# Gates, latents and rope key as two more pairs of tiles with seven part products

## The chip, the cores and the metric

The kernel runs on one core of one Trainium2 chip. The metric is the device time of that core in microseconds (us) from launch to end. The engines are called as in the profile: PE (TensorE, matmul; PEld its weight loads), DVE (VectorE), ACT (ScalarE), POOL (GpSimd) and SP (SyncE, whose queue issues all transfers here). Transfers run on 16 DMA engines.

## The reference

One layer of an encoder over 2048 tokens of width 1024, in float32. What matters here is its input projection:

```
xn   = rms_norm(x, ln_mix_g)                   # 2048 x 1024
proj = xn @ w_in                               # 1024 x 2512
q, k, v, o = proj in four parts of 512         # mLSTM: q and k go through a 3-tap convolution, o through a sigmoid
gates = proj[2048:2064] + b_gates              # 16 per token: input and forget gate, 2 directions, 4 heads
c_q   = rms_norm(proj[2064:2320], q_norm_g)    # latent of the attention queries
c_kv  = rms_norm(proj[2320:2448], kv_norm_g)   # latent of keys and values
k_rope = rotate(proj[2448:2512], cos, sin)     # 64, shared by the heads
```

Then come the chunkwise mLSTM in both directions, the latent attention, the output projection, a gated MLP with a convolution, and a per-layer input embedding.

## The kernel before

A float32 product is made of three products of float32r halves (low by high, high by low, high by high; `mm3`). A split is a cast of the high half on ACT and a subtraction on DVE (`split`, L117: L121 and L124).

**Input projection** (`in_proj`, L187). Loop over 16 tiles of 128 tokens. Per tile: load a tile of the turned x (L224), split it (`split_x`), multiply by the 464 columns of gates, latents and rope key (`nat` and `rest`, 24 matmuls of width 464, L134), multiply by the 512 value columns (`vals`, 24 of width 512), store the values to `v_d` (L294). `rest` scales on ACT, adds the gate bias, sums squares, rotates the rope key in 32-wide pieces on DVE; `finish` applies the norms; `turn_rest` turns the result by four transposes (L283) and stores it to `rest_d` (L288). Beside it run `square` (load rows of x, sum squares on ACT, L235 and L237), which gives the token factors `rcol`; `norm_row` turns eight of them into a row and stores it to `r_d`. From tile 4 on, three times per tile, a step of `work` is taken: `token_sums` (L398) loads x for a block of 1024 tokens, scales it by the row of factors (L429) and makes the token sums of the seven-product scheme, for both blocks; of the first block most are split into SBUF (`op`), the rest and all of the second go to `xo_d`.

**Pairs** (`pairs`, L506). For each of two blocks of 1024 tokens, six pairs of 128-feature tiles of q, k and o. A pair is a 2x2 product by Strassen's scheme: seven part products of 12 matmuls 128x512 each, 84 in all (`prod`, L544), in the banks `fx`, `fy`, `fz`, `fs`. `pair_load` loads the weights two pairs ahead, `pair_prep` makes their sums and splits them one pair ahead; `conv` applies the taps on DVE and the activation on ACT and stores. A function `side(at)` is called between part products and lets other work in: the gate calculation (`gates`, generator, pairs 1 to 4) and, in the last pair, the beginning of the queries (`queries_begin`; in each of two calls four plain-F32 matmuls 128x128, L713).

**What sets the order.** A scheduler orders each engine's instructions when the program is built, from the dependencies and the order of the code; each engine then runs its list in order and waits at semaphores. SP's list holds every transfer: one whose wait isn't met holds all behind it. The transfers take eight semaphores in turn, so that each also waits for the one eight places ahead of it.

## Time and profile before

| | us |
|---|---|
| median of 3 runs (lowest, highest) | 2844.04 (2841.64, 2844.45) |
| span of the profiled execution | 2844.3 |
| PE busy | 2810.8 |
| DVE, ACT, POOL busy | 2133.1, 1580.2, 212.2 |
| input projection, to the first pair's matmul | 189.8 |
| pairs, to the first matmul of the queries | 189.8 to 425.9 |

The page gives busy time per engine. In the rows of a timeline stand the start, the length, the engine, the line, what is written and read, the count and in brackets the idle time before, with what ended it. The pace of back-to-back instructions is the distance of their starts, which is less than the length of one, since they overlap. In the table by windows each row is a stretch of the span.

### The profile page before, as it was taken

The numbers are of one execution on the slowest core, as the hardware profiler recorded it, in microseconds if no ns is written. First come the engines' busy times: TensorE is split into PE (matmuls) and PEld (weight loads), VectorE is DVE, ScalarE is ACT, GpSimd is POOL, SyncE is SP. The second block draws the span as 40 slices with busy tenths as digits, with TensorE's granted clock in tenths as the row PEclk, the third lists the DMA queues.
The fourth block names the chain that finished last, engine by engine and source line by source line (L and its number), as shares of the span: only waits on it lengthen the run. The fifth ranks groups of instructions, "written<-read, shape, count | busy, mean of one in ns | idle before, by whom it ended". The sixth has DMA issues, their size and how long they took to land.

```text
span 2844.3 us, 39914 instructions
## 1 busy us (share of the span) xinstructions
PE 2810.8 (99%) x13932; PEld 2357.0 (83%) x13932; DVE 2133.1 (75%) x3673; ACT 1580.2 (56%) x3072; POOL 212.2 (7%) x331
## 2 busy tenths in 40 slices
PE   9999999999999999999999999999999999999998
PEld 8888888888888888888888888888888788888787
DVE  4877867777787777877778778777778766676777
ACT  6346775556556556655655556655556333254665
POOL 2100000000010000044100000000000000011012
PEclk9999999999999999999999999999999999999999
DMA  8874758554433333579745445567776757575864
GB/s 285 292 244 113 215 170 263 157 169 142 137 122 108 105 99 106 162 239 298 232 148 198 164 170 180 183 209 232 231 239 214 229 194 237 170 265 201 291 198 163
DMA packets 444529, 552.71 MB, mean 194 GB/s; under 512 B 34564, under 2 KB 296744, under 8 KB 444328
## 3 DMA queue, kind: packets, MB, share of 16 engines
q1 hardware_dynamic: 444328, 550.16, 60.2%
q8 instruction: 110, 1.80, 0.3%
q14 instruction: 91, 0.75, 0.1%
HBM read 357.45 MB, written 192.61 MB: 193 GB/s over the span
## 4 chain that ended last, share of the span: by engine, by line
PE 90%; DVE 4%; DMA 3%; issue 1%; ACT 1%; SPq 0%; POOL 0%; ACTq 0%; POOLq 0%; DVEq 0%
PE fy L1709 22%; PE fz L1709 15%; PE fx L1709 14%; PE bk L134 6%; PE ppv L1248 4%; PE tb L1236 3%; PE fy L544 3%; PE fx L544 2%; PE fz L544 2%; PE ppv L1249 2%; PE bk L1171 2%; PE bk L1173 2%; PE bk L1174 2%; PE bk L1172 2%; PE bk L1175 2%; PE fs L134 2%
## 5 line engine op out<-in xcount | busy, mean ns | idle before, releaser
L1709 PE MATMUL fz<-op,fw 128*128 128x512 f32 x1968 | 478.4, 391 | 2.4 <-DVE ug L1694 1.8
L1709 PE MATMUL fx<-op,fw 128*128 128x512 f32 x1968 | 475.9, 390 | 0.0
L1709 PE MATMUL fy<-op,fw 128*128 128x512 f32 x1968 | 475.1, 390 | 0.0
L1709 PEld LDWEIGHTS fz<-op,fw 128*128 128x128 f32 x1968 | 367.1, 188 | 81.1 <-DVE ug L1694 2.2
L1709 PEld LDWEIGHTS fy<-op,fw 128*128 128x128 f32 x1968 | 368.6, 188 | 76.9 <-DVE xt L1694 0.4
L1709 PEld LDWEIGHTS fx<-op,fw 128*128 128x128 f32 x1968 | 368.1, 188 | 76.1
L121 ACT CAST pt<-tb 128x512 fp32r<-128x512 f32 x256 | 146.9, 587 | 213.7 <-PE tb L1236 213.1
L1709 PE MATMUL fy<-op,fwd 128*128 128x512 f32 (+1 forms) x984 | 237.8, 390 | 1.5 <-DVE fh L1694 1.5
L1709 PEld LDWEIGHTS fy<-op,fwd 128*128 128x128 f32 x984 | 182.7, 188 | 39.7 <-DVE fh L1694 1.8
L1176 DVE TENSOR_REDUCE mx<-bk 128x1 f32<-128x512 f32 x256 | 175.2, 685 | 52.7 <-PE bk L1175 50.6
L124 DVE TENSOR_TENSOR pt<-tb,pt 128x512 fp32r<-128x512 f32 x256 | 173.1, 685 | 33.0 <-ACT pt L121 31.4
L1248 PE MATMUL ppv<-pt,kv 128*128 128x512 f32 x512 | 189.0, 407 | 1.0 <-DVE pt L124 1.0
L1193 ACT ACTIVATE pe<-bk,nm 128x512 f32<-128x512 f32 x256 | 174.5, 698 | 17.4 <-DVE nm L1187 15.6
L124 DVE TENSOR_TENSOR fw<-fwr,fw 128x1024 fp32r<-128x1024 f32 x124 | 150.9, 1220 | 35.3 <-ACT fw L121 35.0
L121 ACT CAST op<-opr 128x512 fp32r<-128x512 f32 x201 | 117.7, 620 | 73.0 <-DMA opr<-xo_d 13.2
L1236 PE MATMUL tb<-ident,pe 128*128 128x128 f32 x1024 | 150.9, 273 | 3.1 <-DVE pt L124 3.1
L121 ACT CAST fw<-fwr 128x1024 fp32r<-128x1024 f32 x124 | 129.8, 1050 | 37.5 <-DVE fwr L1683 20.0
L124 DVE TENSOR_TENSOR op<-opr,op 128x512 fp32r<-128x512 f32 x201 | 131.7, 692 | 19.0 <-ACT op L121 18.3
L1249 PE MATMUL ppv<-pt,kv 128*128 128x256 f32 x512 | 144.7, 283 | 0.0
L1236 PEld LDWEIGHTS tb<-ident,pe 128*128 128x128 f32 x1024 | 122.5, 140 | 23.4 <-DVE pt L124 5.4
L121 ACT CAST fw<-hraw 128x1024 fp32r<-128x1024 f32 (+1 forms) x72 | 70.1, 980 | 116.5 <-PE fx L1709 58.9
L1757 DVE SCALAR_TENSOR_TENSOR fgv<-uv,fcw,fgv 128x1024 f32<-128x1024 f32 x88 | 112.7, 1281 | 10.3 <-ACT fgv L1755 9.6
(409 smaller groups left out, 5200.8 us busy)
## 6 DMA issues: line engine op xcount, KB each, us to landing
fwr<-in_w_up SPq DMA_DIRECT2D x66, 512.0 KB, 4.7
fh<-h_d SPq DMA_DIRECT2D x48, 512.0 KB, 3.5
h_d<-fh SPq DMA_DIRECT2D x48, 512.0 KB, 4.3
s_d<-fwr SPq DMA_DIRECT2D x44, 512.0 KB, 3.2
fws<-s_d SPq DMA_DIRECT2D x44, 512.0 KB, 3.5
rw<-row_d SPq DMA_DIRECT2D x32, 512.0 KB, 5.2
tw_d<-tsum SPq DMA_DIRECT2D x60, 256.0 KB, 5.1
opr<-tw_d SPq DMA_DIRECT2D x60, 256.0 KB, 5.3
```

Of the source, the lines that this page charges most:

```text
L121: nc.scalar.copy(hi, src)
L124: (sub or nc.vector).tensor_tensor(lo, src, _f(hi), op=ALU.subtract)
L134: mm = lambda *a, **k: self.nc.tensor.matmul(*a, **k, skip_group_check=more)
L544: nc.tensor.matmul(out, a[:, k * P:(k + 1) * P], parts[lo], start=first, stop=lo == 1 and k == 3, skip_group_check=more)
L1171: mm(ps, ql, kh[:, ks], start=True, stop=False)
L1176: nc.vector.tensor_reduce(s.mx[:, kb:kb + 1], ps, axis=AX.X, op=ALU.max)
L1193: nc.scalar.activation(s.pe[:, kb % 2], s.banks[kb], AF.Exp, bias=s.nm, accum_out=s.rs[:, kb:kb + 1])
L1236: nc.tensor.transpose(t[:, j, :], s.p[kb][:, j * P:(j + 1) * P], self.ident)
L1248: mm(w.ps, vh[:, ks], pts[kb][:, j], start=kt == 0, stop=False, skip_group_check=True)
L1249: mm(w.ps[:, 0], vl[:, ks], pts[kb][:, j, 0], start=False, stop=kt == NT - 1, skip_group_check=True)
L1709: nc.tensor.matmul(out, a[:, k * P:(k + 1) * P], parts[lo][:, cols], start=first, stop=lo == 1 and k == last, skip_group_check=more)
L1757: nc.vector.scalar_tensor_tensor(t, u[:, tap:tap + 2 * SB], self.taps[:, tap, ct:ct + 1], t, op0=ALU.mult, op1=ALU.add)
```

## The change

The 464 columns leave the loop over token tiles. They become two more pairs per block, ahead of the six: the first holds the kv latent and, as its second tile, the first 64 columns (gates and 48 more) beside the 64 of the rope key; the second holds the two tiles of the query latent. A block has 8 pairs, 16 in all. Features now lie on partitions, so nothing is turned: a latent pair's `conv` stores u to `lat_d`, `kr_d` or `gate_d` and squares it; `sums` adds the squares over features by eight plain-F32 matmuls of one column against a constant; `norm_row` makes a row of factors from them (`lr_d`). In block two `rescale` reloads latents and rope key, applies factor and gain, rotates the key on POOL, turns the kv latent for `vv_d` (L699) and stores `rest_d`. `gates` reads its units straight from `gate_d` by 34 small transfers, and runs in pairs 12 to 14.

In the projection only `vals` is left per tile, with two `square`s per tile up to tile 8 and two steps of `work` from tile 5 on. `token_sums` makes the first block only, all but B22 split into SBUF; the second block's sums are in `next_sums`, taken in pairs 1 to 6 (by `side`).

Where the order of the lists moves, three places matter. First PE, at the end of the projection and the start of the pairs (`bk` is the projection's bank; `wsr` and `wsp` the weights of the rest and of the values). Before:

```order
L134 MATMUL bk<-wsr,xh 128x464 x24
L134 MATMUL bk<-wsp,xh 128x512 x30
L283 MATMUL rtp<-ident,nn 128x128 x4
L134 MATMUL bk<-wsp,xh 128x512 x18
L283 MATMUL rtp<-ident,nn 128x128 x4
L544 MATMUL fz<-op,fw_1851 128x512 x2
L629 MATMUL fy<-op,fw_1793 128x512
L544 MATMUL fx<-op,fw_1793 128x512 x4
L544 MATMUL fx<-op,fw_1794 128x512 x4
L544 MATMUL fx<-op,fw_1793 128x512 x4
L544 MATMUL fz<-op,fw_1851 128x512 x10
L544 MATMUL fy<-op,fw_2024 128x512 x4
```

Now:

```order
L139 MATMUL bk<-wsp,xh 128x512 x144
L300 MATMUL tb<-ident,rcol 8x128
L139 MATMUL bk<-wsp,xh 128x512 x120
L489 MATMUL fz<-op,fw_949 128x512 x7
L607 MATMUL fy<-op,fw_907 128x512
L489 MATMUL fx<-op,fw_907 128x512 x4
L489 MATMUL fx<-op,fw_908 128x512 x4
L489 MATMUL fx<-op,fw_907 128x512 x4
L489 MATMUL fz<-op,fw_949 128x512 x5
L489 MATMUL fy<-op,fw_1018 128x512 x4
```

The value tiles now follow each other without the products of width 464 and the transposes between them, and five matmuls instead of ten stand between `fx` and the `fy` that reads its copy.

Second, SP's queue where the first token loads (`xsr`) and the row of factors (`rrow`) are issued, up to the load of x tile 7 (the last row). Before:

```order
L235 DMA x_row<-in_x 128x1024 x3
L412 DMA xsr<-in_x_turned 128x1024
L148 DMA rrow<-r_d 128x1024
L412 DMA xsr<-in_x_turned 128x1024
L288 DMA rest_d<-rt 512x1x128
L412 DMA xsr<-in_x_turned 128x1024 x2
L420 DMA xo_d<-xsr 128x512
L294 DMA v_d<-vo 128x512
L277 DMA vv_d<-nn 128x128
L224 DMA x_t<-in_x_turned 128x8x128
```

Now:

```order
L240 DMA v_d<-vo 128x512
L303 DMA r_d<-r_439 8x128
L334 DMA xsr<-in_x_turned 128x1024 x2
L240 DMA v_d<-vo 128x512
L153 DMA rrow<-r_d 128x1024
L334 DMA xsr<-in_x_turned 128x1024 x2
L212 DMA x_t<-in_x_turned 128x8x128
```

The value store just ahead of x tile 7 was that of tile 4 and is now that of tile 5 (the second `v_d` row).

Third, DVE between two subtractions of x tiles (`xh<-x_t,xh`) while the first block's token sums are made. Before, around tile 7:

```order
L459 TENSOR_TENSOR xsr<-xsr 128x512
L269 TENSOR_TENSOR nn<-sc_848 128x32
L293 TENSOR_SCALAR vo<-bk,rcol 128x512
L270 COPY nn<-nn 128x64
L274 SCALAR_TENSOR_TENSOR nn<-rs,rsr,gn 128x256
L124 TENSOR_TENSOR xh<-x_t,xh 128x1024
L124 TENSOR_TENSOR op<-xsr,op 128x512
L450 TENSOR_TENSOR xsr<-xsr 128x512
L124 TENSOR_TENSOR op<-xsr,op 128x512
L253 TENSOR_TENSOR gt<-rs,bg 128x8 x2
```

Now, from tile 8 to tile 9:

```order
L129 TENSOR_TENSOR xh<-x_t,xh 128x1024
L354 TENSOR_TENSOR xsr<-xsr 128x512
L129 TENSOR_TENSOR op<-xsr,op 128x512
L350 SCALAR_TENSOR_TENSOR xsr<-xsr,gcol,rrow 128x1024
L129 TENSOR_TENSOR op<-xsr,op 128x512
L350 SCALAR_TENSOR_TENSOR xsr<-xsr,gcol,rrow 128x1024
L357 TENSOR_TENSOR xsr<-xsr 128x512
L129 TENSOR_TENSOR op<-xsr,op 128x512
L359 TENSOR_TENSOR xsr<-xsr 128x512
L129 TENSOR_TENSOR op<-xsr,op 128x512
L363 TENSOR_TENSOR xsr<-xsr 128x512
L129 TENSOR_TENSOR xh<-x_t,xh 128x1024
```

The small operations of `rest` and `finish` are gone, and whole quarters of the token sums stand between one tile's subtraction and the next.

The diff, cut to its core:

```diff
@@ in_proj @@
-        def rest(st, ps):
-            whole = self.at(f"t{st % 2}", [P, NREST], name="rs")
-            nc.scalar.activation(whole, ps[:, :NREST], AF.Copy, scale=rcol[:, st:st + 1])
-            for i, o in ((0, st), (8, NT - 1 - st)):
-                nc.vector.tensor_tensor(self.gt[:, i:i + 8, o], whole[:, i:i + 8], bg[:, i:i + 8], op=ALU.add)
-            rs = whole[:, 16:NREST]
-            sc = self.at(next(srot), [P, 6, 32], name="sc6")
-            nc.sync.dma_start(sc[:, 0:2], d["rope"][st * P:(st + 1) * P])
-            cos, sin, tt = sc[:, 0], sc[:, 1], sc[:, 2:6]
-            nn = nq[st] = self.at(f"t{2 + st % 2}", [P, 512], name="nn")
-            ssq = self.stat(2, "ssq2")
...
-        def vals(st):
-            ps = nat(st, wv, 512)
-            t = self.at("t4", [P, 512], name="vo")
-            nc.vector.tensor_scalar(t, ps, rcol[:, st:st + 1], None, op0=ALU.mult)
+                self.mm3(ps, x[:, 0, kt], x[:, 1, kt], wv[kt][:, 0], wv[kt][:, 1], kt == 0, kt == KT - 1)
+            t = self.at(f"t{4 + st % 2}", [P, 512], name="vo")
+            if st < 5:
+                nc.vector.tensor_scalar(t, ps, rcol[:, st:st + 1], None, op0=ALU.mult)
+            else:
+                nc.scalar.activation(t, ps, AF.Copy, scale=rcol[:, st:st + 1])
             nc.sync.dma_start(self.v_d[st], t)
...
         work = chain(self.token_sums(), self.pair_begin())
-        for st in range(2, NT):
+        sq = iter(range(1, NT))
+        for st in range(1, NT):
+            if st + 1 < NT:
+                load_x(st + 1)
+                split_x(st + 1)
+            for _ in range(2):
+                if (q := next(sq, None)) is not None:
+                    square(q)
...
+            vals(st)
+            if st == 4:
+                x_row_factors(0)
+            if st == 10:
+                x_row_factors(1)
                 self.pair_load(0)
-            if st + 2 < NT:
-                load_x(st + 2)
-            if st + 1 < NT:
-                split_x(st + 1)
-            rest(st, nat(st, wr, NREST))
-            if st < 5:
-                for q in range(4 * st - 4, 4 * st):
-                    square(q)
-            if st > 3:
+            if st > 4:
                 next(work, None)
...
+    NPB = 8
+    COLS = [(OFF_R + 272, None), (OFF_R + 16, OFF_R + 144)] + [(256 * j, 256 * j + P) for j in (0, 1, 2, 3, 6, 7)]
+    def load_w(self, t, j, e):
+        c = self.COLS[j][e]
+        for o, n, c in ((0, P, c),) if c is not None else ((0, 64, OFF_R), (64, 64, OFF_R + 400)):
+            self.nc.sync.dma_start(t[:, :, o:o + n], self.d["w_in"][0, :, c:c + n].rearrange("(k p) c -> p k c", p=P))
...
@@ token_sums @@
+        rr = self.row_bcast(self.at("x11", [P, 2 * SB], name="rrow"), self.r_d[0:2 * SB], 2 * SB)
+        yield
+        for k in range(4):
             a, b = nxt
-            if i < 7:
-                nxt = load(i + 1)
+            if k < 3:
+                nxt = load(k + 1)
             for t, kt in ((a, k), (b, k + 4)):
-                nc.vector.scalar_tensor_tensor(t, t, self.gcol[:, kt:kt + 1], rr[:, blk], op0=ALU.mult, op1=ALU.mult)
-            store(blk, "B22", k, b[:, H])
-            if blk:
-                store(blk, "B11", k, a[:, L])
-                store(blk, "B21", k, b[:, L])
-                yield
-                tt(a[:, H], a[:, H], a[:, L], op=ALU.subtract)
-                store(blk, "T1", k, a[:, H])
-                c = self.at(("u2", "w3")[k % 2], [P, 2, SB], name="xsc")
-                tt(c[:, 0], b[:, H], a[:, H], op=ALU.subtract)
-                store(blk, "T2", k, c[:, 0])
-                yield
-                tt(c[:, 1], c[:, 0], a[:, L], op=ALU.subtract)
-                store(blk, "T3", k, c[:, 1])
-                t4 = self.at("t7", [P, SB], name="xsd")
-                tt(t4, b[:, L], c[:, 0], op=ALU.subtract)
-                store(blk, "T4", k, t4)
-                yield
-                continue
+                nc.vector.scalar_tensor_tensor(t, t, self.gcol[:, kt:kt + 1], rr, op0=ALU.mult, op1=ALU.mult)
+            self.store_op(0, "B22", k, b[:, H])
...
+    def next_sums(self):
+        nc = self.nc
+        tt = nc.vector.tensor_tensor
+        rr = []
+        for e in range(2):
+            t = self.at(f"t{4 + e}", [P, SB], name="rrow")
+            rr.append(self.row_bcast(t, self.r_d[(2 + e) * SB:(3 + e) * SB], SB))
+        for k in range(4):
+            q = []
+            for i in range(4):
+                q.append(self.at(f"t{i}", [P, SB], name="xsq"))
+                nc.sync.dma_start(q[i], self.d["x_turned"][:, k + i // 2 * 4, (2 + i % 2) * SB:(3 + i % 2) * SB])
+            al, ah, bl, bh = q
+            def scale(t, i):
+                kt = k + i // 2 * 4
+                nc.vector.scalar_tensor_tensor(t, t, self.gcol[:, kt:kt + 1], rr[i % 2], op0=ALU.mult, op1=ALU.mult)
+            yield
+            scale(al, 0)
+            self.store_op(1, "B11", k, al)
+            scale(ah, 1)
+            tt(ah, ah, al, op=ALU.subtract)
+            self.store_op(1, "T1", k, ah)
+            yield
+            scale(bh, 3)
+            self.store_op(1, "B22", k, bh)
+            t2 = self.at("t7", [P, SB], name="xsd")
+            tt(t2, bh, ah, op=ALU.subtract)
+            self.store_op(1, "T2", k, t2)
+            yield
+            scale(bl, 2)
+            self.store_op(1, "B21", k, bl)
+            tt(al, t2, al, op=ALU.subtract)
+            self.store_op(1, "T3", k, al)
+            yield
+            tt(bl, bl, t2, op=ALU.subtract)
+            self.store_op(1, "T4", k, bl)
...
@@ pairs @@
+            if s.pr < 0:
+                u = u[:, 1:1 + 2 * SB]
+                if s.pr == -2 and half:
+                    nc.sync.dma_start(self.kr_d[:, ts], u[64:P])
+                    nc.sync.dma_start(self.gate_d[:, ts], u[0:16])
+                    return
+                nc.sync.dma_start(self.lat_d[2 if s.pr == -2 else half, :, ts], u)
+                s.sq[half] = sq = self.at(("w7", "w11")[half], [P, 2 * SB], name="lsq")
+                nc.scalar.activation(sq, u, AF.Square)
+                if s.pr == -1 and not half:
+                    tt(sq, sq, s.sq[1], op=ALU.add)
+                return
             if s.pr > 3:
...
+        def sums(s, bank):
+            ps = bank[:, 0:8]
+            for t in range(8):
+                nc.tensor.matmul(ps[:, t:t + 1], s.sq[0][:, t * P:(t + 1) * P], self.nhalf[:, 0:1], start=True, stop=True)
+            ssq = self.stat(8, "lssq")
+            nc.vector.tensor_copy(ssq, ps)
+            s.rc = self.rsq(ssq, 8, -2.0 / (P if s.pr == -2 else 2 * P))
...
+                if j in (2, 3) and at == 1:
+                    sums(lat[j - 2], bank)
+                if j in (2, 3) and at == 2:
+                    self.norm_row(bank[0:8, 0:P], lat[j - 2].rc, self.lr_d[j - 2], blk)
+                if 0 < i < 6 and at % 2:
+                    next(ahead, None)
+                if (i, at) == (6, 1):
+                    for _ in ahead:
+                        pass
+                if NPB < i < NPB + 4:
+                    next(scaled, None)
+                if NPB + 4 <= i < NPB + 7 and at != 3:
                     next(gates, None)
-                if i == 11:
-                    self.queries_begin(at, prev.spare if at % 2 else s.spare)
+                if i == N - 1:
+                    self.queries_begin(at, bank)
...
@@ rescale @@
+    def rescale(self, blk):
+        nc, d = self.nc, self.d
+        V, G = nc.vector, nc.gpsimd
+        halves = [slice((2 * blk + h) * SB, (2 * blk + h + 1) * SB) for h in range(2)]
+        def load(tag, src):
+            t = self.at(tag, [P, SB], name="rsp")
+            nc.sync.dma_start(t, src)
+            return t
+        def scale(t, n, row):
+            V.scalar_tensor_tensor(t, t, self.lgain[:, n:n + 1], row, op0=ALU.mult, op1=ALU.mult)
+            nc.sync.dma_start(self.rest_d[:, n, ts], t)
+        for ts in halves:
+            row = self.row_bcast(self.at("t5", [P, SB], name="rrow"), self.lr_d[0][ts], SB)
+            kv = load("t0", self.lat_d[2, :, ts])
+            cos, sin = [load(f"t{2 + i}", d["rope_keys"][:, i, ts]) for i in range(2)]
+            a, b = [self.at(("t1", "t4")[i], [P, SB], name="rsk") for i in range(2)]
+            both = lambda p: self.kr_d[p:p + 32, ts].unsqueeze(0).broadcast_to([2, 32, SB])
+            for e in range(2):
+                for t, p in ((a, 32 * e), (b, 32 - 32 * e)):
+                    for r in range(2):
+                        nc.sync.dma_start(t[64 * r + 32 * e:64 * r + 32 * e + 32], self.kr_d[p:p + 32, ts])
+            yield
+            scale(kv, 2, row)
+            G.tensor_tensor(a, a, cos, op=ALU.mult)
+            G.tensor_tensor(b, b, sin, op=ALU.mult)
+            G.tensor_tensor(a, a, b, op=ALU.add)
+            nc.sync.dma_start(self.rest_d[:, 3, ts], a)
+            yield
+            pt = self.gate_bank.rearrange("p (k t) -> p k t", t=P)
+            for k in range(4):
+                nc.tensor.transpose(pt[:, k], kv[:, k * P:(k + 1) * P], self.ident)
+            o = self.at("t7", [P, 4, P], name="vvo")
+            nc.scalar.copy(o, pt)
+            nc.sync.dma_start(self.vv_d[:, ts.start // P:ts.start // P + 4], o)
+            yield
+        for ts in halves:
+            row = self.row_bcast(self.at("t5", [P, SB], name="rrow"), self.lr_d[1][ts], SB)
...
@@ gates @@
+        raw = []
+        for f in range(2):
+            g = tl()
+            for r in range(2):
+                src = self.gate_d[8 * r + 4 * f:8 * r + 4 * f + 4].rearrange("h (c t) -> c h t", t=P)
+                for c in range(NT) if r else (None,):
+                    if r:
+                        nc.sync.dma_start(g[64 + 4 * (NT - 1 - c):64 + 4 * (NT - c)], src[c])
+                    else:
+                        nc.sync.dma_start(g[0:64], src)
+            raw.append(g)
         def to_units(f):
-            g = tl()
-            V.tensor_copy(g.rearrange("p (r c h) -> p r h c", r=2, h=4), gt[:, :, f])
-            yield
-            pt = pbank()
-            nc.tensor.transpose(pt, g, self.ident)
             o = tl()
-            flip(o, pt)
+            flip(o, raw[f])
+            V.tensor_scalar(o, o, self.gbias[:, f:f + 1], None, op0=ALU.add)
...
```

229 lines of the change are left out of this document (80 added, 149 removed).

## The prediction

> **What bounds the kernel now.** I read the page first, for the engines and the clock.
>
> ```profile
> span 2844.3 us, 39914 instructions
> PE 2810.8 (99%) x13932; PEld 2357.0 (83%) x13932; DVE 2133.1 (75%) x3673; ACT 1580.2 (56%) x3072; POOL 212.2 (7%) x331
> PEclk9999999999999999999999999999999999999999
> ```
>
> TensorE (PE) is busy for all but 33 us of the span, at full clock. So the time changes in two ways only: by PE work that goes or comes, and by new holes in PE. Everything the change touches lies in the first 426 us (the input projection and the pairs), so the table by windows comes next: length, then PE, PEld, DVE, ACT, POOL busy, clock, DMA share, GB/s.
>
> ```profile
> 20.00:40.00 20.00, 20.00 (x96) 16.99 (x95) 10.64 (x32) 11.97 (x24) 5.73 (x12) 1.00 0.81 257
> 80.00:120.00 40.00, 37.27 (x178) 31.52 (x177) 36.03 (x82) 17.61 (x39) 3.53 (x8) 1.00 0.90 283
> 120.00:160.00 40.00, 40.00 (x190) 34.16 (x190) 30.13 (x71) 9.54 (x22) 6.56 (x7) 1.00 0.98 319
> 200.00:240.00 40.00, 40.00 (x178) 32.85 (x177) 28.26 (x58) 22.39 (x34) 0.00 (x0) 1.00 0.28 81
> 240.00:280.00 40.00, 39.07 (x176) 31.91 (x175) 32.61 (x67) 27.96 (x45) 0.00 (x0) 1.00 0.53 149
> ```
>
> The reader should see three things. PE is full in the projection although the DMA engines are already 81% to 98% busy there and VectorE (DVE) up to 90%. In the pairs DMA is at 28% to 53%. So the projection hides two loads just behind PE, and it is the stage that the change shortens on PE. The timeline of PE gives its paces (start, length, line, count, idle before):
>
> ```profile
> 15.66 5.28 PE L134 MATMUL bk<-wsr,xh 128*128 128x464 f32 x24 [1.31 <-DVE xh L124]
> 20.78 11.07 PE L134 MATMUL bk<-wsp,xh 128*128 128x512 f32 x48
> 31.69 0.60 PE L283 MATMUL rtp<-ident,nn 128*128 128x128 f32 x4
> 32.04 2.13 PE L134 MATMUL bk<-wsr,xh 128*128 128x464 f32 x9
> ...
> 189.83 0.71 PE L544 MATMUL fz<-op,fw 128*128 128x512 f32 x2
> ...
> 197.14 3.06 PE L544 MATMUL fy<-op,fw 128*128 128x512 f32 x12 [1.34 <-ACT fy L631]
> 200.03 2.88 PE L544 MATMUL fx<-op,fw 128*128 128x512 f32 x12
> 202.75 2.88 PE L544 MATMUL fy<-op,fw 128*128 128x512 f32 x12
> ...
> 405.58 1.13 PE L713 MATMUL fs<-ukvt,uqt 128*128 128x128 f32 x8
> 406.46 2.55 PE L544 MATMUL fy<-op,fwd 128*128 128x512 f32 x10
> ```
>
> From start to start: 24 value matmuls take (31.69 - 20.78)/2 = 5.455 us; 24 of width 464 take 5.12; four transposes 0.35; twelve of a pair 2.72 (200.03 to 202.75), so a pair of 84 takes 19.04.
>
> **The change part by part: PE.** The 464-wide product and its 64 transposes go, so the value tiles follow each other. Tile 0 is paced by weights that arrive and are split, as now; tile 1 waited for its split x until 15.66. About 0.2 MB more weights stand ahead of that x (512 columns for 464), so I put it at 16.2. With no new hole, tile k starts at 16.2 + 5.455 (k - 1) and tile 15 ends at 98.0, where the projection now ends at 189.83: **-91.8 us**.
>
> Four pairs come: 4 x 19.04 = **+76.2**. The sums of squares are 32 plain-F32 matmuls. L713 shows that the trace has such a matmul as two (four in the loop, eight in the row), at (406.46 - 405.58)/8 = 0.11 us each; 64 x 0.11 = **+7.0**. One moving column instead of 128 could make them cheaper, so 3.5 to 7.4. Sixteen transposes of the kv latent at 0.35/4 are **+1.4**, four short ones for the row factors about +0.5, two in the gates go (-0.2). At the start of pair 0 only five matmuls instead of ten stand between the first product and the one that waits for ACT's copy (1.34 us idle now), 5 x 0.227 = **+1.1**. Net on PE without new holes: -91.8 + 86.0 = **-5.8 us**. The Strassen saving is thus small: 88 us of products and transposes are exchanged for 76, and 10 of the 12 go to bookkeeping; the rest of the -5.8 is idle time in the old projection.
>
> **The change part by part: what must keep up.** The projection shrinks from 190 us to 98, so its loads come at nearly twice the pace. Price of a transfer, by two windows (60 to 80 and 205 to 250 us; packets, MB, share of 16 engines); the third row is the start, 5 to 20 us:
>
> ```profile
> q1 hardware_dynamic: 3492, 5.87, 86.4%
> q1 hardware_dynamic: 8663, 4.61, 36.8%
> DMA packets 4272, 5.54 MB, mean 369 GB/s; under 512 B 429, under 2 KB 3014, under 8 KB 4272
> ```
>
> That is 16 x 20 x 0.864/3492 = 79 ns per packet of 1681 bytes, and 31 ns per packet of 532: 8 ns + 0.042 ns per byte. An x tile (1024 packets of 512 bytes, 64 on each of the 16 engines) is then 1.90 us, a 4 KB-row load of 512 KB 1.45, a value store 0.76. Through tile 6 each tile brings one x tile, two x rows and a value store: 1.90 + 2.90 + 0.76 = 5.56 us of all engines, against 5.455 of PE. So DMA is at its limit with no backlog allowed.
>
> [...]
>
> Then comes the place that decides. SP issues in order, and a load that stands behind a value store waits for that store's tile:
>
> ```profile
> SPq L294 <- DVE vo L293: 20.6, 9, 4.9
> L251 ACT ACTIVATE rs<-bk,rcol 128x464 f32<-128x464 f32 x12 | 7.7, 645 | 17.1 <-PE bk L134 17.1
> 104.75 0.32 SPq L294 DMA_DIRECT2D v_d<-vo  x1
> 105.59 0.60 SPq L224 DMA_DIRECT2D x_t<-in_x_turned  x1
> DMA to landing us min/median/max: 4.3/4.4/4.5
> DMA to landing us min/median/max: 5.0/5.1/5.2
> ```
>
> (Waits of SP; ACT's scaling of a product; two issues of the SP timeline; landing of an x tile, then of the row of factors.) Now x tile 7 stands behind the value store of tile 4, two tiles of 10.9 us ahead of its use. In the change it stands behind the store of tile 5, one tile of 5.455 us ahead, with the row of factors and two token loads between. Tile 5 ends at 43.5. Its scaling is ACT's in the change (0.65 us, with two squares before it), so the store goes at 44.4 to 46.5. Behind it are 0.76 + 1.45 + 2.90 + 1.90 = 7.0 us of DMA, then 2.5 us from issue to landing beyond the transfer (4.4 - 1.9): landing at about 54.5. Cast and subtraction take 2.3 more, where PE wants the tile at 48.9. With some of the token work ahead of it, tile 7 starts near 58: **9 us** of hole. Low end, with nothing queued: 44.4 + 1.5 + 4.4 + 2.3 = 52.6, 4 us; high end 11.
>
> From the row of factors on (about 50 us), DVE and ACT do the first block's token sums in what used to be 11 us per tile. Prices, from starts on DVE and groups on ACT:
>
> ```profile
> 83.49 1.22 DVE L124 TENSOR_TENSOR xh<-x_t,xh 128x1024 fp32r<-128x1024 f32 x1
> 84.62 0.68 DVE L124 TENSOR_TENSOR op<-xsr,op 128x512 fp32r<-128x512 f32 x1
> 85.22 0.69 DVE L450 TENSOR_TENSOR xsr<-xsr 128x512 f32<-128x512 f32 x1
> ...
> 106.16 2.48 DVE L429 SCALAR_TENSOR_TENSOR xsr<-xsr,gcol,rrow 128x1024 f32<-128x1024 f32 x2
> 108.55 0.69 DVE L124 TENSOR_TENSOR op<-xsr,op 128x512 fp32r<-128x512 f32 x1
> L121 ACT CAST xh<-x_t 128x1024 fp32r<-128x1024 f32 x10 | 10.5, 1046 | 21.6 <-PE bk L134 9.9 <-DVE vo L293 6.6 <-DMA x_t<-in_x_turned 5.1
> L121 ACT CAST op<-xsr 128x512 fp32r<-128x512 f32 x16 | 9.8, 621 | 27.3 <-DVE xsr L429 15.9 <-DVE xsr L453 7.8 <-DVE xsr L450 3.5
> L237 ACT ACTIVATE x_row<-x_row 128x1024 f32<-128x1024 f32 x4 | 4.2, 1056 | 4.0 <-DMA x_row<-in_x 4.0
> L237 ACT ACTIVATION_READ_ACCUMULATOR x_row<-x_row 128x1 f32 x4 | 0.8, 188 | 0.0
> ```
>
> So DVE's paces are 1.13 (1024 wide), 0.60 (512) and 1.20 (scaling). By the new order of DVE, between the subtraction of tile 7 and that of tile 8 lie 6.5 us of paces (its own included), 8.3 to tile 9, 3.5 to tile 10, 5.9 to 11, 7.1 to 12, then 2.9, 2.3 and 4.1. Against 5.455 that adds 1.0 + 2.8 + 0.1 = 4 us, DVE never waiting: hole 13 in all. But each half operand is cast by ACT and then subtracted by DVE, so each queue also waits for the other. Tile 8, with tile 7's x subtracted at 58.4: ACT has five casts (0.62), two squares (1.06 + 0.19) and the x cast (1.05), 6.6 us from 57.2, and waits some 2.4 for DVE's sums: 66.2, subtracted 67.4, while tile 7 ended at 63.9: 3.5 us. Tile 9: two squares, two scalings, four casts and the x cast, 7.4 us, and 4.9 of waits for the four sums that DVE makes between them: 78.5, subtracted 79.7, while tile 8 ended at 72.9: 6.8. In the same way 0.9 at tile 11 and 2.3 at 12, with tile 7's 9.6 in this walk: 23 in all. I take **+19** for the new holes, nearer to the walk, with 5 and 27 as ends. After tile 12 the list is light, so the projection ends at about 117 and DMA has caught up.
>
> Costed at nothing: the second block's sums (32 DVE operations of 0.60, 19 us, over five pairs). The latent pairs have no taps, and the fullest pair then counts 17 us of DVE against 19; without that cover some 1 to 3 us. Rescaling and the gates lie in block two, where a pair has the DVE load of the 200 to 280 windows. The gates' 34 small loads hold SP for about 34 x 0.32 = 11 us ahead of the last pair's weights only, a pair of 19 us before their use; without that cover 3 us.
>
> **Sum.** 2844.3 - 5.8 + 19 = 2857.5; the profiled execution is 0.3 above the median and inside the three runs, so **2857 us**.
>
> **Rivals.** *The loads keep up* (not slower): x tile 7 lands unqueued, the DVE and ACT lists interleave as the scheduler meant, hole 4 to 5: 2843. For it, the start moved 369 GB/s, and DVE reached 90% in the 80 to 120 window with only 2.7 us lost on PE. Against it, that one tile alone gives 4 in its best case. It decides when the hole stays under 11 us (no measurable change), and a gain over 0.2% (5.7 us, about what can be told apart here) needs no hole at all and sums at the low price: 2844.3 - 5.8 - 3.5 = 2835. *The pairs run short too*: hole of 22 in the projection, plus DVE falling behind in pairs 1 to 4, where 17 us of paces meet waits for PE and ACT; 240 to 280 already lost 0.9 us at 32.6 of 40. 2 us per pair gives 2844 - 6 + 22 + 8 = 2868. *Late gates*: the gates now wait for two round trips through DRAM and end just before the queries; PE stands in order behind their transposes. PE's waits in the pairs are now these two alone, so I give it 3 to 5 us, 2861.
>
> ```profile
> PE fy L544 <- ACT fy L631: 1.3, 1, 1.3
> PE fy L544 <- DVE uv L562: 0.9, 1, 0.9
> ```
>
>
> **How the numbers follow.** Forecast (hole 12 to 25, nothing else): 0.58. Loads keep up: 0.22, of which 0.07 faster by over 0.2%. Pairs short: 0.14. Late gates: 0.06. Slower by over 0.2% (above 2849.7): 0.58 + 0.14 + 0.06 = 0.78; same 0.15; faster 0.07. Range 2846 to 2868: it leaves out most of the first rival below and half of the second above. The forecast's own is 2850 to 2864.
>
> **What would show it.** Right: PE idle on L139 released by DVE xh of 15 us or more between 45 and 100 us, the first piece of 7 us or more near 50; the SP queue showing x tile 7 issued right after the value store of tile 5; pairs beginning near 117 and lasting 320 us. Wrong: pairs beginning before 108 (the loads keep up), or idle on L489 beyond 5 us (the pairs bind). If the sums of squares show under 0.06 us each, the PE term was too dear by 3.

## The result, and the profile after

The changed kernel takes 2887.47 us (median of four runs, 2882.19 to 2892.12) where the kernel before, on the same chip, takes 2844.24: a ratio of 1.0153, 95% interval 1.0139 to 1.0168. It is slower, as forecast, but by 43 us, not 13. The profiled execution has a span of 2890.3 us, 46.0 above the profiled execution before. The head of its page:

```profile
span 2890.3 us, 39794 instructions
PE 2825.9 (98%) x13902; PEld 2358.3 (82%) x13902; DVE 2142.3 (74%) x3544; ACT 1589.0 (55%) x3029; POOL 228.4 (8%) x319
```

and the ends of the two stages in PE's timeline (start, length, line, count, idle before):

```profile
59.00 13.20 PE L139 MATMUL bk<-wsp,xh 128*128 128x512 f32 x48 [10.07 <-DVE xh L129]
77.85 13.95 PE L139 MATMUL bk<-wsp,xh 128*128 128x512 f32 x48 [5.65 <-DVE xh L129]
97.61 22.06 PE L139 MATMUL bk<-wsp,xh 128*128 128x512 f32 x96 [0.22 <-DVE xh L129]
119.51 1.75 PE L489 MATMUL fz<-op,fw 128*128 128x512 f32 x7
...
469.27 1.56 PE L139 MATMUL gb<-woa,uvs 128*128 128x512 f32 x6
```

The first pair starts at 119.51 (189.83 before), the query projection at 469.27. Before, it stood at

```profile
425.85 1.56 PE L134 MATMUL gb<-woa,uvs 128*128 128x512 f32 x6
```

So the projection became 70.3 us shorter (forecast: 91.8 less 19, 72.8), the pairs went from 236.0 to 349.8 us, 113.7 more (forecast: 86.0), and 2.6 us were lost after them. The first term held. The second is 28 us off, and the windows show where (length, then PE, PEld, DVE, ACT, POOL busy, clock, DMA share, GB/s):

```profile
40.00:60.00 20.00, 9.93 (x42) 7.90 (x41) 9.50 (x11) 9.32 (x15) 1.49 (x5) 0.83 0.87 290
60.00:80.00 20.00, 14.35 (x52) 11.35 (x51) 16.13 (x23) 14.24 (x24) 10.91 (x9) 0.84 0.84 274
...
280.00:320.00 40.00, 36.21 (x161) 29.41 (x159) 29.77 (x40) 25.47 (x40) 4.62 (x3) 1.00 0.82 247
320.00:360.00 40.00, 34.35 (x157) 28.14 (x157) 13.57 (x21) 11.77 (x17) 7.82 (x6) 0.96 0.71 210
360.00:400.00 40.00, 36.62 (x157) 29.24 (x157) 25.57 (x39) 18.43 (x23) 9.99 (x7) 0.91 0.60 174
```

From 280 to 400 all engines stand at times. DVE is busy for only 13.57 of 40 us from 320 to 360, and the granted clock falls to 0.91. These are pairs 8 to 12; the rescaling's instructions run from 300 to 406. Who waits for whom there: PE, over the whole span (total, times, longest),

```profile
PE fs L699 <- DVE rsp L677: 8.8, 3, 4.8
PE fs L300 <- POOL rsr L149: 4.2, 2, 2.8
```

DVE, by groups of instructions from 276 to 470 (busy, mean ns, idle before),

```profile
L677 DVE SCALAR_TENSOR_TENSOR rsp<-rsp,lgain,rrow 128x512 f32<-128x512 f32 x12 | 8.9, 750 | 18.4 <-DMA rsp<-lat_d 16.4 <-DMA rsk<-kr_d 1.9
```

and SP's queue from 276 to 400:

```profile
SPq L695 <- POOL rsk L694: 21.3, 3, 8.9
```

They read from the bottom up. SP, which issues in order, stands 21.3 us in three waits at L695, the store of the rotated rope key, because POOL has not finished it. Behind that store stand the loads of the next half's latents. DVE then stands 18.4 us at L677 for those loads. Behind L677 stand the splits of the next pair's operands, and PE stands 8.8 us at L699, the transposes of what L677 scales. One such chain in SP's timeline (start, length of the issue):

```profile
322.46 0.43 SPq L502 DMA_DIRECT2D lat_d<-ug  x1
331.92 0.32 SPq L695 DMA_DIRECT2D rest_d<-rsk  x1
...
333.32 0.98 SPq L673 DMA_DIRECT2D rsp<-lat_d  x2
```

what it waited for, on POOL, and its end, on DVE:

```profile
329.73 2.16 POOL L694 TENSOR_TENSOR rsk<-rsk 128x512 f32<-128x512 f32 x1
```

```profile
337.98 1.41 DVE L677 SCALAR_TENSOR_TENSOR rsp<-rsp,lgain,rrow 128x512 f32<-128x512 f32 x2 [6.65 <-DMA rsp<-lat_d]
```

SP issues nothing from 322.9 to 331.9, when POOL's last instruction of that half ends. DVE gets the loads at 338, 4.7 us after their issue.

POOL was not only slow. Its three instructions take some 5 us in a row, but before the second and the third of these stores it also stood in its own order at L147, which makes the factors of the latents, until DVE had copied PE's sums of squares:

```profile
325.21 0.20 POOL L147 TENSOR_SCALAR rsm<-lssq 128x8 f32<-128x8 f32 x1 [12.88 <-DVE lssq L563]
362.49 1.13 POOL L147 TENSOR_SCALAR rsm<-lssq 128x8 f32<-128x8 f32 x1 [10.97 <-DVE lssq L563]
```

Behind the second of these the rotation goes on at 365.31, though the last of its loads was issued by 353.9. And PE's sums come behind PE's wait at L699, so the chain closes on itself. How much this part costs alone was not tried.

That is a reading of waits. The experiments test it. Times are given as microseconds above the kernel before on the same chip, where the changed kernel has +43.2 (1.0139 to 1.0168); one interval is about 4 us to each side. Single profiles spread too: seven kernels whose projection is that of the change (the change itself among them) end it between 116.7 and 119.7, and five whose pairs are unchanged need 344.5 to 349.8 us for them. A smaller difference in one stage says nothing.

### The profile page after: what moved, and what is told of

It is laid out like the page before. It is cut to its first block, busy times and chain, and to the rows that moved or that the text cites. A ratio compares the mean times of both kernels' runs of the same rounds, so it can differ in the third digit from the quotient of the medians.

```text
span 2890.3 us, 39794 instructions
## 1 busy us (share of the span) xinstructions
PE 2825.9 (98%) x13902; PEld 2358.3 (82%) x13902; DVE 2142.3 (74%) x3544; ACT 1589.0 (55%) x3029; POOL 228.4 (8%) x319
## 4 chain that ended last, share of the span: by engine, by line
PE 75%; DMA 6%; DVE 5%; ACT 3%; issue 1%; SPq 1%; POOL 1%; ACTq 0%; POOLq 0%; DVEq 0%
PE fy L1741 21%; PE fz L1741 14%; PE fx L1741 14%; PE ppv L1280 3%; PE tb L1268 3%; PE ppv L1281 2%; PE bk L1203 2%; PE bk L1205 2%; PE bk L1206 2%; PE bk L1207 2%; PE bk L1204 2%; PE fs L139 2%; DMA rsp<-lat_d 1%; PE mb L1142 1%; PE mb L1143 1%
## 5 line engine op out<-in xcount | busy, mean ns | idle before, releaser
L1741 PEld LDWEIGHTS fy<-op,fw 128*128 128x128 f32 x1968 | 368.5, 188 | 78.5 <-DVE fh L1726 1.4
L1741 PEld LDWEIGHTS fy<-op,fwd 128*128 128x128 f32 x984 | 182.8, 188 | 39.9 <-DVE fh L1726 1.9
L129 DVE TENSOR_TENSOR fw<-fwr,fw 128x1024 fp32r<-128x1024 f32 x136 | 166.1, 1224 | 38.0 <-ACT fw L126 36.8
L126 ACT CAST fw<-fwr 128x1024 fp32r<-128x1024 f32 x136 | 142.6, 1051 | 63.2 <-DVE fwr L1715 20.2
L129 DVE TENSOR_TENSOR fwd<-fwr,fwd 128x512 fp32r<-128x512 f32 x60 | 43.1, 719 | 114.2 <-ACT fwd L126 113.8
```

The costliest lines, as they stand in the source:

```text
L126: nc.scalar.copy(hi, src)
L129: (sub or nc.vector).tensor_tensor(lo, src, _f(hi), op=ALU.subtract)
L1741: nc.tensor.matmul(out, a[:, k * P:(k + 1) * P], parts[lo][:, cols], start=first, stop=lo == 1 and k == last, skip_group_check=more)
```

## The experiments: the pairs

**Without the rescaling.** The loop bodies of `rescale` become copies from memory to memory.

```diff
-            scale(kv, 2, row)
-            G.tensor_tensor(a, a, cos, op=ALU.mult)
...
+            nc.sync.dma_start(self.rest_d[:, 2, ts], self.lat_d[2, :, ts])
...
```

> The rescaling of keys, values and latents in block two is left out: no loads for it, no multiplications on DVE, no rope rotation on POOL, no transposes on PE; plain copies from memory to memory stand at the same places (so the latents, the rope keys and the turned key latents stay unscaled). The sums of squares, the factor rows and the gates stay. Theory (the rescaling is what made the pairs longer than forecast: 8.8 us of PE waits by name, the late operands behind the DVE's own waits for loads of about 5 us, and the clock that falls after them): about 25 us less than the changed kernel, 2862 (2855 to 2868). Rival A (DVE and ACT are simply full in block two with splits, sums and gates, and the rescaling only stands in the way by name): the 8.8 us and 16 transposes of about 0.16 us go, 2876 (2872 to 2880). Rival B (the prediction: the rescaling costs nothing): 2885 to 2889.

Measured 2858.2, +12.5 (1.0042, 1.0027 to 1.0057): 31 us less, the theory's side. Its pairs:

```profile
116.92 1.75 PE L489 MATMUL fz<-op,fw 128*128 128x512 f32 x7
...
436.98 1.56 PE L139 MATMUL gb<-woa,uvs 128*128 128x512 f32 x6
```

320.1 us, the length that the forecast named for the pairs. (The terms of its sum, 236.0 and 86.0, make 322.0, or 320.6 without the 1.4 us of transposes that this run leaves out.) So the gates, the sums of squares, the factor rows and the second block's token sums together cost what the forecast said. The rescaling costs about 30 us, where the forecast had 1.4 us of transposes.

**PE reads nothing fresh.** The 16 transposes and the four of the factor rows take a constant.

```diff
-                    self.norm_row(bank[0:8, 0:P], lat[j - 2].rc, self.lr_d[j - 2], blk)
+                    self.norm_row(bank[0:8, 0:P], self.rcol[:, 8 * blk:8 * blk + 8], self.lr_d[j - 2], blk)
...
-                nc.tensor.transpose(pt[:, k], kv[:, k * P:(k + 1) * P], self.ident)
+                nc.tensor.transpose(pt[:, k], self.ident, self.ident)
```

> The 16 transposes of the rescaled key latents and the four of the factor rows of the latents read a constant that has long been there instead of the fresh tile; everything else (loads, DVE, POOL, stores, the number of matmuls) stays. The turned key latents and the factor rows of the latents hold wrong numbers. Theory (TensorE works in order, so what costs is that it stands at these two lines): the named waits of 8.8 us and, of the 4.2 us at the factor rows, the 4.2 in the pairs go, and with them most of the slow clock behind them, 2871 (2866 to 2875). Rival (the late link is the DVE, which stands in order at its own waits for the loads, so that the next pair's operands are late anyway and TensorE waits at the next product instead): 2881 to 2888, with idle time at L489 in place of that at L699.

Measured 2877.25, +31.5 (1.0095 to 1.0125); the pairs take 339.0. Both are half right. About 11 us come back, somewhat less than the 13.0 that PE had stood at the two lines, and the other 19 stay: DVE still stands 19.0 us at L677 and SP 18.0 at L695. What PE waits for by name is a third of the cost.

**Without POOL's rope rotation.** Three instructions in each half are left out.

```diff
-            G.tensor_tensor(a, a, cos, op=ALU.mult)
-            G.tensor_tensor(b, b, sin, op=ALU.mult)
-            G.tensor_tensor(a, a, b, op=ALU.add)
```

> The three POOL instructions of the rope rotation in each of the four halves are left out, so the rope keys are stored unrotated; every load, store, transpose and DVE instruction stays. The rescaling as a whole was shown to cost 30 us of the pairs. Theory 1 (SP's queue is the cause: the store of the rotated rope key waits there for POOL, about 5.3 us, and the loads of the next half and of the next pair's weights stand behind it; POOL at work also slows the DVE's adds from 0.69 to 1.67 us): 10 to 16 us less than the changed kernel, 2874 (2871 to 2878). Theory 2 (the round trip of each step's own loads, about 5 us against a step of 2.7 us, is the cause, POOL only stands beside it): 2882 to 2888.

Measured 2872.31, +28.0 (1.0088 to 1.0118), pairs 331.2: 15 to 19 us back, by leaving out 18 us of work on an engine that is busy for 8% of the span. Of SP's waits in the same stretch, 276 to 400, only 1.1 us are now at the rope key's store (for its loads); the longest are

```profile
SPq L678 <- DVE rsp L677: 19.1, 11, 4.3
SPq L466 <- DVE op L129: 9.6, 11, 2.0
```

**The rope rotation on DVE.** The same three instructions, `V.` for `G.`.

> The 12 instructions of the rope rotation run on DVE instead of POOL (about 0.69 us each there, 1.3 to 1.75 on POOL); all else as in the changed kernel. Leaving them out gave 15 us. Theory 1 (SP's store waits for POOL's chain, about 5 us per half, with all later loads behind it): the chain is 2 us on DVE, 6 to 12 us less, 2878 (2874 to 2882). Theory 2 (what counts is which engine stands behind the small rope-key loads: on DVE, which also prepares the next pair's operands, the wait for these loads is worse than on POOL, which does nothing else): no gain or slower, 2886 to 2896.

Measured 2882.42, +37.2 (1.0113 to 1.0143), pairs 346.0: between the two theories, and the interval just meets that of the change. DVE makes each in 0.69 us, yet SP still stands at the store:

```profile
SPq L678 <- DVE rsp L677: 19.7, 9, 3.6
SPq L695 <- DVE rsk L694: 12.9, 4, 5.2
```

The rotation comes in its turn in DVE's queue, between L677 and the sums and splits of the next operands. In the first half it lasts 4.3 us there from its first start to its end, against 4.7 on POOL: a faster engine with a queue of its own work ends it hardly sooner. So what seems to count is when the store may go, not how long the rotation takes; the next two runs test that.

**Spread.** Loads two sides ahead, 24 steps from pair 8 on, five small loads for eight, the store and the factor row one side later.

```diff
-                if NPB < i < NPB + 4:
+                if (i, at) >= (NPB, 7) and i < N - 2:
                     next(scaled, None)
...
-            yield
-            scale(kv, 2, row)
+            yield
+            yield
+            scale(kv, 2, r)
```

> The same rescaling, spread: each step's loads are issued two sides ahead of their use, the rope key comes in five loads instead of eight, its rotated form is stored a side after the transposes, both halves of the query latents are loaded ahead into their own buffers, and the 24 steps run from the seventh side of pair 8 to the second of pair 12 instead of 20 steps in pairs 9 to 11; the factor row of the latents is turned one side later. All work is kept. Theory (the 30 us are waits of DVE, SP and TensorE for steps that follow each other faster than a load's round trip, not work): pairs last about 324 us instead of 350, 2862 (2857 to 2870). Rival (the rescaling's own work on DVE, about 9 us, and the loads' share of the DMA engines cost it wherever they stand): 2874 or more.

Measured 2878.22, +33.9 (1.0100 to 1.0133), pairs 343.6. The rival's number, though not for its reason (the next run has the same work). A side is 2.7 us; POOL's three instructions take 3.9 to 5.6 us from the first start to the last end in this run, and start when their own loads have landed. So one side later is too soon, and SP stands again, with the early loads behind it:

```profile
SPq L706 <- POOL rsk L697: 13.8, 4, 4.7
```

**Spread and interleaved.** The query latents of a half are loaded and scaled between POOL's rotation and its store; 28 steps, four loads for the rope key, the gates a pair later.

```diff
             G.tensor_tensor(a, a, b, op=ALU.add)
-            nc.sync.dma_start(self.rest_d[:, 3, ts], a)
             yield
...
-        for ts in halves:
-            row = self.row_bcast(self.at("t5", [P, SB], name="rrow"), self.lr_d[1][ts], SB)
-            raw = [load(f"t{e}", self.lat_d[e, :, ts]) for e in range(2)]
+            r = row(1, ts)
+            raw = [load(("t0", "t7")[e], self.lat_d[e, :, ts]) for e in range(2)]
+            yield
             yield
             for e in range(2):
-                scale(raw[e], e, row)
+                scale(raw[e], e, r)
+            nc.sync.dma_start(self.rest_d[:, 3, ts], a)
             yield
```

> All work is kept. The rescaling takes 28 steps instead of 20, from the seventh side of pair 8 to the sixth of pair 12; each load stands two sides ahead of its use; per half the query latents follow the key latents (into other buffers), and the rotated rope key is stored three sides after POOL began on it instead of one, so that SP's queue should not stand for POOL; the rope key comes in four loads of 64 partitions instead of eight of 32 (its two halves are stored swapped as well, by two more stores per block); the gates follow in pairs 13 and 14. Theory (the 30 us are waits in SP's, DVE's and TensorE's order, SP's for POOL above all): pairs last about 326 us instead of 350, 2864 (2858 to 2871). Rival (as in the run that only spread it, the queue of SP with its many small transfers holds the loads back whatever the spacing): 2876 or more.

Measured 2870.48, +25.3 (1.0069 to 1.0103), pairs 331.3: all work kept, and as much back as without the rotation. SP's waits have no line for POOL any more. PE's waits in this kernel (L703 and L680 are the transposes and the scaling):

```profile
PE fs L703 <- DVE rsp L680: 5.1, 3, 2.3
PE fy L490 <- DVE uv L456: 3.6, 2, 2.2
```

By SP's wait at that store these kernels stand in two groups: with 21.3, 13.8 and 12.9 us of it the pairs take 349.8, 343.6 and 346.0, which is the spread of unchanged pairs or just under it; with 1.1 and none, 331.2 and 331.3. This run and the one before share the spacing and nearly the same loads; what differs most is when the store goes and what stands ahead of it, and that is 12 us of pairs. The spread alone takes 9 us off the time; how they divide between its parts was not tried. Of the last 11 us to 320.1, 8.7 stand in these two rows, and the transposes are 1.4.

## The experiments: the projection

**x tiles two tiles ahead**, in three buffers.

```diff
-            xq[st] = self.at(f"u{st % 2}", [P, KT, P], name="x_t")
+            xq[st] = self.at(("u0", "u1", "w3")[st % 3] if st < 12 else f"u{st % 2}", [P, KT, P], name="x_t")
...
+            if st + 2 < NT:
+                load_x(st + 2)
             if st + 1 < NT:
-                load_x(st + 1)
                 split_x(st + 1)
```

> In the projection x tiles are loaded two tiles ahead, into three buffers in turn instead of two; nothing else. Theory (as predicted: the x tiles of the holes are late because their load stands in SP's queue behind a value store and the token sums' loads): the waits of 10.1 and 5.7 us at L139 and the about 5 us by which the following tiles run at a lower clock go, projection ends near 100, 2869 (2864 to 2874). Rival (the x tile stands in the queues of ACT and DVE behind the token sums that wait for their factor row until 51.7, so an earlier load helps little): a hole of 6 to 8 us stays at tile 7, 2880 to 2885.

Measured 2884.96, +39.2 (1.0122 to 1.0153), projection to 116.9: within the spread of an unchanged one. The theory, which is the prediction's, falls. The hole moves to tile 8 and is smaller, but others come (3.17 and 2.21 us at tiles 10 and 13, some 2 ahead of tile 5), as PE's and DVE's timelines show for the first:

```profile
64.27 13.18 PE L139 MATMUL bk<-wsp,xh 128*128 128x512 f32 x48 [5.71 <-DVE xh L129]
```

```profile
55.20 2.48 DVE L352 SCALAR_TENSOR_TENSOR xsr<-xsr,gcol,rrow 128x1024 f32<-128x1024 f32 x2 [4.54 <-DMA rrow<-r_d]
```

No load of an x tile is what ACT or DVE wait for there. DVE stood at the first scaling of the token sums until the row of factors landed, 5.8 us after its issue at 49.39, and the casts and subtractions of x stood behind.

**Token sums two tiles later**, on top of the former.

```diff
-            if st > 4:
+            if st == 5:
+                next(work)
+            if st > 6:
                 next(work, None)
```

> x tiles two tiles ahead as in the run before (which gave about 4 us), and the token sums' arithmetic begins two tiles later: after tile 5 only their loads and the factor row are issued, the steps follow from tile 7 on, two per tile. Theory 1 (DVE stood in order at its first scaling until the factor row landed at 55.2, with the x tile's cast and subtraction behind it): no wait over 2 us is left at L139 before tile 9, projection ends near 108, 2876 (2872 to 2880). Theory 2 (memory traffic limits the x tiles): the holes move to other tiles and keep about 10 us in sum, 2884 to 2888.

Measured 2877.96, +33.7 (1.0104 to 1.0134), projection to 112.4: 4 to 7 us below the spread. The time is theory 1's, its stage is not: forecast near 108, and holes of 2.45, 3.54 and 1.59 us remain at tiles 8, 10 and 14. That they move to other tiles is theory 2's.

**Without the loads of x rows.** All squares read the first row tile.

```diff
+        nc.sync.dma_start(row0, d["x"][0, 0:P, :])
...
-            nc.sync.dma_start(t, d["x"][0, st * P:(st + 1) * P, :])
-            nc.scalar.activation(t, t, AF.Square, accum_out=sq)
+            nc.scalar.activation(t, row0, AF.Square, accum_out=sq)
```

> In the projection the 16 loads of x rows for the sums of squares are left out but for one: every square reads the first row tile (so the row factors are those of the first 128 tokens throughout). ACT's squares, the x tiles, the token sums and the stores stay; about 7.9 MB less is loaded before 75 us. Theory 1 (the memory traffic is what makes the x tiles and the factor row late: 0.97 and 0.87 of the 16 DMA engines' time from 20 to 60 us): the holes of 10.1 and 5.7 us fall under 3 us in sum, projection ends near 100 to 103, 2870 (2866 to 2874). Theory 2 (ACT and DVE in order, with the casts of x tiles behind the token sums' casts, is the cause): a hole of 5 us or more stays and the projection ends at 112 or later, 2880 or more.

Measured 2872.02, +27.7 (1.0083 to 1.0113), projection to 105.1, theory 1. One hole is left in the timeline, although tile 1 began 4 us later than in the change:

```profile
19.48 16.62 PE L139 MATMUL bk<-wsp,xh 128*128 128x512 f32 x72 [0.17 <-DVE xh L129]
...
41.83 32.92 PE L139 MATMUL bk<-wsp,xh 128*128 128x512 f32 x144
77.34 27.89 PE L139 MATMUL bk<-wsp,xh 128*128 128x512 f32 x120 [2.48 <-DVE xh L129]
```

Its windows show DMA at 0.65 from 40 to 60, where the change has 0.87:

```profile
40.00:60.00 20.00, 20.00 (x90) 16.47 (x89) 13.96 (x16) 9.24 (x14) 0.00 (x0) 1.00 0.65 204
```

So leaving out 7.9 MB of rows gives back some 14 us of the stage. The rows are not issued faster than before: the kernel before issues them from 5.8 to 61.8 us, the change from 5.9 to 69.2. What is new beside them are the x tiles and the value stores at twice the pace.

The run takes more away than traffic. ACT's squares no longer wait for rows (the last ends at 34.5 us instead of 78.5), and the order moved: x tile 7 is issued at 44.34, ahead of the value store of tile 5 at 48.30. For the traffic speak two things. An earlier load alone moved the end of the stage by no more than the spread in the run with x tiles ahead. And x tile 7 is there at most 3.8 us after its issue, when ACT takes it up at 48.17, where in the change it took 7.9 (48.36 to 56.23). That the traffic is the cause is thus likely, and not shown apart from ACT's shorter list. The order in the queues decides which tile pays and, by the run before, some 5 us of the 14.

**Holes filled.** 80 and 40 transposes of a constant before tiles 7 and 9.

```diff
-            vals(st)
+            vals(st, {7: 80, 9: 40}.get(st, 0))
```

> 80 transposes of a constant are put before the products of tile 7 and 40 before those of tile 9, into the bank that the products then overwrite: at about 0.13 us each, 10 and 5 us, as long as the holes there. Nothing else changes. Theory (after a hole the granted clock is low for some us: the 48 matmuls behind each hole took 13.2 and 13.9 us instead of 10.9): the clock stays at 1.00 through 60 to 100, the holes themselves stay as long, about 5 us less, 2882 (2880 to 2885). Rival (the clock falls for another reason, or the transposes do not count as work): 2887 or more.

Measured 2884.93, +39.2 (1.0122 to 1.0156, which meets the interval of the change), projection to 117.3, within the spread. The first half of the theory holds, the second does not:

```profile
49.17 8.89 PE L231 MATMUL bk<-ident 128*128 128x128 f32 x80
59.50 5.76 PE L139 MATMUL bk<-wsp,xh 128*128 128x512 f32 x24 [1.43 <-DVE xh L129]
66.06 5.75 PE L139 MATMUL bk<-wsp,xh 128*128 128x512 f32 x24 [0.81 <-DVE xh L129]
71.64 4.53 PE L231 MATMUL bk<-ident 128*128 128x128 f32 x40
77.85 11.18 PE L139 MATMUL bk<-wsp,xh 128*128 128x512 f32 x48 [1.68 <-DVE xh L129]
```

The clock stays at 1.00 and the 48 products take 11.18 us instead of 13.95. But tile 9 starts at 77.85 as in the change: its x tile was not split earlier, and PE's faster products only lengthened the wait before it. Here the slow clock cost nothing, since the next tile was awaited anyway.

**All repairs together**, with the rows of the second eight tiles loaded one per tile (into one buffer; the second block's row of factors is made two tiles later).

```diff
-            for _ in range(2):
+            for _ in range(2 if st < 5 else 1):
                 if (q := next(sq, None)) is not None:
```

> All work is kept: the spread and interleaved rescaling, x tiles two tiles ahead, the token sums' arithmetic two tiles later, and the x rows for the second eight squares loaded one per tile from tile 5 on instead of two (about 2 MB of loads moved from 45 to 65 us to 65 to 95). Theory (the causes add up: about 23 us from the pairs, 9.5 from the projection as measured, some 3 from the spread rows): 2852 (2846 to 2860), still not below the kernel before, whose 2844 no sum of these reaches. Rival (the gains overlap, since shorter waits in the projection only move traffic into the first pairs): 2862 or more.

Measured 2865.72, +20.5 (1.0052 to 1.0082), projection to 113.7, pairs 332.8: the rival. Half of the loss is repaired with all work kept, and the kernel before stays faster. The spread rows gave nothing; holes of 3.10 and 3.11 us came at tiles 13 and 14 instead.

**Neither cause.** The edits of the runs without the rescaling and without the loads of x rows, in one kernel.

> Both suspects are left out at once: the rescaling's work (plain copies from memory to memory in its place) and all but one load of the x rows. What stays of the change is its products, sums, gates and token sums. Theory (two separate causes, the rescaling's waits in the pairs and the memory traffic in the projection, which together account for the whole loss): the gains of the two runs, 30 and 15 us, add up, 2842 (2838 to 2847), projection ending near 105 and pairs lasting 320 us, no measurable difference from the kernel before. Rival (they overlap, or a third cost of some size is left): 2850 or more.

Measured 2843.65, -1.3 against the kernel before: 0.9995, 0.9985 to 1.0004.

```profile
77.42 30.31 PE L139 MATMUL bk<-wsp,xh 128*128 128x512 f32 x120 [3.98 <-DVE xh L129]
...
425.90 1.56 PE L139 MATMUL gb<-woa,uvs 128*128 128x512 f32 x6
```

The projection ends at 107.6, the pairs take 318.3, and the query projection starts at 425.90, 0.05 us from where it stood before the change. The two gains (30.7 and 15.5) add up to 46 of which 44.5 come. Together they account for the loss against the kernel before. Something is left against PE's own sum: the projection still ends 9.6 us after the 98.0 of the forecast without holes.

## Why the prediction was right and wrong

**PE's own terms held.** In the kernel without the rescaling the sums of squares read

```profile
312.76 1.84 PE L561 MATMUL fs<-nhalf,lsq 128*128 128x1 f32 x16
314.46 3.02 PE L489 MATMUL fz<-op,fw 128*128 128x512 f32 x12
```

1.70 us from start to start, 0.106 each, priced at 0.11 (half of that for one column, the prediction's low end, was an estimate that no run bears out), and the pairs take 320.1 us, the number given. The net without holes was -5.8; the last run, in which some holes stay, gives -1.3.

**The projection held in size, and its mechanism in part.** Forecast end 117, measured 119.5. For tile 7 the chain ran as forecast: the value store of tile 5, then the load of the x tile, then ACT's cast when it has landed, forecast for about 54.5:

```profile
46.54 0.33 SPq L240 DMA_DIRECT2D v_d<-vo  x1
48.36 0.55 SPq L212 DMA_DIRECT2D x_t<-in_x_turned  x1
56.23 1.04 ACT L126 CAST xh<-x_t 128x1024 fp32r<-128x1024 f32 x1 [0.17 <-DMA x_t<-in_x_turned]
```

The hole there was put at 9 and is 10.07. But this place is not the one that decides, as the prediction called it: loaded a tile earlier, the x tile is no longer waited for, DVE's wait for the row of factors takes its place, and the stage ends no sooner. The hole at tile 9 was put at 6.8 and is 5.65. The 3.5 at tile 8, 0.9 at 11 and 2.3 at 12 are not there (0.22 at most); some 4.8 us of slower products after the two holes (13.20 and 13.95 for 11.18) are there instead, which the prediction had no term for. That these two errors nearly cancel is luck. The sentence ahead of that place, that 5.56 us of transfers meet 5.455 us of PE with no backlog allowed, is what the run without the row loads bears out, as far as that run goes.

**The step that failed** is one clause of what was costed at nothing: "Rescaling and the gates lie in block two, where a pair has the DVE load of the 200 to 280 windows." It holds for the gates. For the rescaling it added up DVE's busy time and found room. It gave no account of a step's chain: small loads on SP, POOL behind them and behind PE's sums of squares, a store on SP that waits for POOL, the next loads behind it, DVE in order behind those, PE in order behind DVE. The price was about 30 us, not the 1.4 of the transposes; leaving POOL's rotation out, or moving its store further behind it with the next loads ahead, gave back 15 and 18 of them. The prediction had walked just such a chain in the projection, and did not walk it here.

**The rivals.** "The pairs run short too" named the right stage and 8 us, but put it in pairs 1 to 4, by DVE's throughput; in those pairs little is lost (from 120 to 280 PE is busy for 39.2 to 40 of each 40 us in the kernel without rescaling, 38.6 to 39.9 in the change), and it came in pairs 9 to 12 by waits. "Late gates" came to 0.8 us, one wait of PE in the gates. "The loads keep up" did not.

**The signs.** Idle on L139 of 15 us (15.7 from 45 to 100), the x tile's load behind the store of tile 5, and pairs beginning near 117 came as forecast, their 320 us did not. "Idle on L489 beyond 5 us" as the sign of binding pairs looked at the wrong line: PE's waits there add up to 4.9, just under the bound, because PE stood 13.0 us at the transposes L699 and L300 between the products.

## What to carry to other kernels

Work costed at nothing needs its chain walked, not its busy time added: list for each step what every in-order queue issues behind its waits, above all the queue that issues loads behind a store. A store that waits for another engine should be issued as many steps later as that engine needs, its own waits included, with the loads of the next step ahead of it; that gave back 18 of 30 us with no work removed. And a stage that is shortened to half keeps its traffic: compare bytes per tile with time per tile first, since the reorderings tried here recovered 4 to 7 us and leaving bytes out some 14.

## What the runs showed of the hardware

**Two of DVE's adds took 1.67 us while POOL worked, where others like them took 0.69.** In the change's DVE timeline, against POOL's at the same time:

```profile
309.51 1.67 DVE L432 TENSOR_TENSOR fwr<-fwr 128x512 f32<-128x512 f32 x1
311.21 1.67 DVE L433 TENSOR_TENSOR fwr<-fwr 128x512 f32<-128x512 f32 x1
312.91 0.69 DVE L436 TENSOR_TENSOR fwr<-fwr 128x512 f32<-128x512 f32 x1
```

```profile
308.88 1.75 POOL L692 TENSOR_TENSOR rsk<-rsk,rsp 128x512 f32<-128x512 f32 x1
310.70 1.62 POOL L694 TENSOR_TENSOR rsk<-rsk 128x512 f32<-128x512 f32 x1
```

Of all seven of L432 in this stretch, in the change and then without POOL's rotation:

```profile
L432 DVE TENSOR_TENSOR fwr<-fwr 128x512 f32<-128x512 f32 x7 | 5.8, 829 | 0.2
```

```profile
L432 DVE TENSOR_TENSOR fwr<-fwr 128x512 f32<-128x512 f32 x7 | 4.8, 691 | 0.2
```

Each of the two starts while an instruction of POOL runs and ends some 0.55 us after it (311.18 after 310.63, 312.88 after 312.32). Not every add beside POOL took longer: L455 at 330.66 took 0.68 us while POOL's L694 ran from 329.73 to 331.89. Over L432 and its neighbour L433 (828 ns in the mean, 688 without the rotation) it is about 2 us of DVE here. What makes the two slow was not tested.

**The clock after a hole.** In the change 48 products took 13.20 us behind the hole of 10.07 and 13.95 behind that of 5.65, 2.0 and 2.8 us longer than 11.18, with the granted clock at 0.84 from 60 to 80 us and at 0.90 from 80 to 100. Behind holes of 2.45 us (tile 8 with the later token sums; clock 0.84 from 60 to 80, where the hole of 3.54 lies too) and 3.11 us (tile 14 with all repairs; 0.91 from 100 to 120) 48 products took 12.77, 1.6 us longer. Behind one of 3.17 us (tile 10 with x tiles ahead; 1.00 from 80 to 100) 24 products took 5.74, as for tile 4 of the change with no hole before it (5.75). So the length of a hole alone does not say here whether the products behind it are slow, and what else decides it no run shows.
